# Strassen's seven products in gate/up and fewer of them in down, with h transposed through DRAM and VectorE's work ordered by an estimate of its queue

## The chip, the cores and the metric

The kernel runs on one NeuronCore of a Trainium2 chip. The metric is the device time of one execution in microseconds, lower is better. The time before is the median of three runs.

## The reference

One decoder layer on x with 256 tokens and 2048 features, in float32: a half-step SwiGLU FFN, a mixer (attention and convolution side by side, one projection in and one out), and a second half-step FFN, each followed by a LayerNorm over the residual sum. Cut to what the change touches:

```python
def swiglu_ffn(x, w_gate, w_up, w_down):
    h = jax.nn.silu(x @ w_gate) * (x @ w_up)
    return h @ w_down

x = layer_norm(ALPHA * x + 0.5 * swiglu_ffn(x, gate1, up1, down1), ln1_g, ln1_b)
...
x = layer_norm(ALPHA * x + 0.5 * swiglu_ffn(x, gate2, up2, down2), ln3_g, ln3_b)
```

The hidden width is 5632. Nearly all the arithmetic is in these two FFNs.

## The kernel before, in words

**Precision.** Every float32 operand is split into a high part (a copy rounded to float32r, made by ScalarE) and a low part (the difference, made by VectorE). A product of two operands is three matmuls: high times high, high times low, low times high (`mm3`, lines 547 to 550). The stationary operand is a 128x128 block of activations (features by tokens), the moving one 128x512 of weights.

**Weight tiles.** All weights are read once, in tiles of 128x1024 (512 KB). SyncE (SP) loads them into four `raw` buffers. ScalarE writes `hi` (L204), VectorE `lo` (L207), or GpSimd for some tiles of the mixer. Finished pairs wait in a ring of eight (`RING`); TensorE takes them in order with `take` and frees them with `release`. `ahead` makes tiles up to seven ahead of the one in use (`LEAD`), and is called in `step`, once after every tile's matmuls. The program is written out in one order per engine by this class (`Steps`), so each engine's queue is fixed when the program is built. Work that is due some steps later is put down with `at`. `vector` and `tensor` keep an estimate of VectorE's backlog, which before the change decides only how many taps of the convolution are put in.

**Gate/up.** The hidden columns go in groups of 256 (`JG` = 2 blocks of 128): a tile pair of gate and up columns gives a PSUM bank of 128 tokens by 512 for each of the two token blocks. A group takes 8 tiles, that is 8 K pairs of 256 features: 2 token blocks x 2 K blocks x 3 = 12 matmuls per tile (`token_mm`, `token_group`). There are 22 groups in each FFN, cut into three parts of 8, 8 and 6 groups (`PARTS`), with the down stage of each part behind its gate/up stage. The first two groups of the first FFN are woven (`first_groups`).

**h.** For each group (`group`, lines 818 to 857) ScalarE applies silu, VectorE multiplies (L825), then VectorE transposes 32x32 blocks: four calls of `turn`, one per step, each with four STREAM_TRANSPOSE (L832) that write to other partitions, 16 per group. Then h is split into `hh` and `hl` (L841, L842).

**Down.** In the first two parts (`by_sums`, lines 728 to 807) K pairs are taken for two column chunks at once. Here K pair, two token blocks and two column chunks make 2x2 blocks on each side. A K pair of kind C is done plainly, with 8 products (24 matmuls); one of kind S by Strassen's scheme in Winograd's form, with 7 products of block sums (21 matmuls). `KINDS` gives the kinds: three S of eight. For an S pair the two weight tiles become four ring entries, made by VectorE's sums of blocks (`rest`, lines 159 to 184): the first block pair as it is, two sums, the other tile with one block replaced, and one last sum. The seven products go to seven PSUM banks; VectorE joins them at the end of the stage (`shared`, `add`). The third part uses the plain way for all tiles (`tokens_by`).

Of the kernel before, what the change touches and what calls it, by code (L numbers as in the profile page):

```python
# [18 lines left out]
P = 128  # L19
# [6 lines left out]
KINDS = ("CSCSCSCC", "CSCSCSCC", None)  # L26
BLOCKS = {"S": 7, "C": 4}
JG = 2
# [14 lines left out]
BEHIND = 7  # L43
LAST = 8
# [22 lines left out]
class Steps:  # L67
# [6 lines left out]
    def __init__(self, nc, pool, sources, head, pooled, xT, x_raw, xcat):  # L74
        self.nc, self.pool, self.sources, self.head, self.pooled = nc, pool, sources, head, pooled
        self.xT, self.x_raw, self.xcat = xT, x_raw, xcat
        self.loaded = self.open = self.opened = self.whole = self.done = self.used = self.now = 0
        self.jobs, self.ready, self.pending = [], {}, []
        self.later, self.background, self.backlog = [], None, 0.0
        self.most = len(sources)  # L80
# [23 lines left out]
    def load(self):  # L104
        while self.open < RAW_BUFS and self.loaded < len(self.sources):
            n = self.loaded
            if n < 4:
# [8 lines left out]
            if isinstance(self.sources[n], tuple):  # L116
                if self.opened == 2:
                    return
                self.load_set(n)
                continue  # L120
# [6 lines left out]
    def load_set(self, n):  # L127

        raws = [self.raw(), self.extra.tile([P, 1024], F32, tag="rawx", name=f"rawx{n}", bufs=2)]
        self.opened += 1  # L130
# [3 lines left out]
        self.jobs += [(n, raws, self.first), (n + 3, raws, self.rest)]  # L134

    def upper(self, n, raw):

        pair = [self.pool.tile([P, 1024], F32R, tag=t, name=f"{t}{n}", bufs=RING) for t in ("hi", "lo")]
        hi, lo = (t[:, : raw.shape[1]] for t in pair)
        self.nc.scalar.copy(hi, raw)  # L140

        def lower():
            self.nc.vector.tensor_tensor(out=lo, in0=raw, in1=hi.bitcast(F32), op=ALU.subtract)
            self.vector(1.16, 1.3)
# [10 lines left out]

    def first(self, n, raws):
        raws.append(self.upper(n, raws[0]))

    def rest(self, last, raws):

        n = last - 2
        a, b = ([r[:, :512], r[:, 512:]] for r in raws[:2])
        zero = raws[2]
        sub = self.nc.vector.tensor_tensor
        self.flush(1)
        t = self.extra.tile([P, 1024], F32, tag="sum", name=f"sum{n}", bufs=1)
        sub(out=t[:, :512], in0=b[0], in1=a[0], op=ALU.subtract)
        sub(out=t[:, 512:], in0=b[1], in1=t[:, :512], op=ALU.subtract)
        one = self.upper(n, t)
        sub(out=b[0], in0=b[1], in1=b[0], op=ALU.subtract)  # L170
        two = self.upper(n + 1, raws[1])
        self.flush()
        zero()
        sub(out=a[1], in0=a[1], in1=t[:, 512:], op=ALU.subtract)
        self.vector(2.4, 0.3)
        three = self.upper(n + 2, a[1])

        def ended():
            three()
            self.open -= 1  # L180
            self.opened -= 1
            self.load()

        self.pending = [one, two, ended]

    def split(self):
# [7 lines left out]
        elif n is None:  # L194
            nc.scalar.copy(at[:, :, 0, :], raw)
            nc.vector.tensor_tensor(out=at[:, :, 1, :], in0=raw, in1=at[:, :, 0, :].bitcast(F32), op=ALU.subtract)
        else:
# [19 lines left out]
    def ahead(self, most):  # L217
        while most > 0 and self.jobs:
# [5 lines left out]
            most -= 1  # L224

# [35 lines left out]
    def step(self, us=2.6):  # L261
        self.now += 1
        self.tensor(us)
        for after in (False, True):
# [4 lines left out]
            if not after:  # L269
                self.ahead(2)  # L270
# [5 lines left out]
def hybrid_layer(  # L276
# [8 lines left out]
    act = ctx.enter_context(tc.tile_pool(name="act", bufs=1))  # L285
    psA = ctx.enter_context(tc.tile_pool(name="psA", bufs=2, space=PSUM))
# [6 lines left out]

    def add_ffn(wu, wd):
        for (j0, j1), kinds in zip(PARTS, KINDS):
            for g in range(j0 // JG, j1 // JG):
                sources.extend(wu[g, q, h] for q in range(4) for h in range(2))
            pairs = [divmod(t, 2) for t in range(j0 // 2, j1 // 2)]
            if kinds is None:
                sources.extend(wd[c, g, h] for c in range(NC_) for g, h in pairs)  # L300
                continue
            for c in range(0, NC_, 2):
                for kind, (g, h) in zip(kinds, pairs):
                    both = (wd[c, g, h], wd[c + 1, g, h])
# [1013 lines left out]
```

## Time and profile before

| what | value |
|---|---|
| median of three runs | 1701.65 us (1701.25 to 1701.83) |
| the profiled execution | 1702.42 us |
| its span in the profile | 1700.6 us |
| mean granted clock of TensorE | 0.998 |
| loads from HBM | 332.86 MB, 197 GB/s over the span |
| VectorE: low parts of 1024 columns (L207) | 487 of them, 591.3 us busy |
| VectorE: transposes (L832) | 704, 212.7 us busy |

PE is TensorE, PEld its weight loads, DVE VectorE, ACT ScalarE, POOL GpSimd. Busy time is the time covered by an engine's instruction bars. Where bars overlap, the cost of one instruction is the step from its start to the next start, not the length of its bar. In a row of the groups, "out<-in" are the program's tile names: `grp` is a PSUM bank of gate/up, `sum` one of the products of sums, `acc` one of the plain down way, `xcat` the split x, `hh` and `hl` the split h, `hi` and `lo` the split weights.

### The profile page before, as it was taken

Reading aid. Unit: us, or ns where it says so; the run is one execution under the profiler, and the core shown is the slowest. Engines: PE = TensorE matmul, PEld = TensorE weight load, DVE = VectorE, ACT = ScalarE, POOL = GpSimd, SP = SyncE. Lnnn points to the kernel's source line nnn. Section 1 sums busy time; section 2 is a strip of 40 time slices with the busy share of each in tenths; the row PEclk is TensorE's granted clock in tenths of the full one; section 3 lists DMA queues with packets and bytes.
Section 4 is the critical chain, followed back from the end, with each engine's and each line's share of the span. In section 5 each row is a group of like instructions: output and inputs, shape, how many; then the busy total and the mean of one; then the engine's idle time right before and its main releaser. Section 6 shows DMA issues by size and latency. Waiting matters only on the chain.

```text
span 1700.6 us, 21870 instructions
## 1 busy us (share of the span) xinstructions
PE 1687.1 (99%) x7785; PEld 1402.5 (82%) x7785; DVE 1344.6 (79%) x2305; ACT 847.6 (50%) x1112; POOL 206.3 (12%) x116
## 2 busy tenths in 40 slices
PE   9999999999999999999999999999999999999997
PEld 7888888888888888888888888888888888888886
DVE  6877897777897777658888788988977778977766
ACT  6454454444454444477665465544544444544441
POOL 0000000000000000168996200000000000000000
PEclk9999999999999999999999999999999999999999
DMA  8766467656467566556655557665576664576672
GB/s 307 248 218 209 139 209 238 194 194 204 136 207 247 190 197 194 171 174 190 204 177 160 190 184 240 212 204 169 196 230 190 193 210 159 190 234 197 198 235 75
DMA packets 96303, 336.41 MB, mean 198 GB/s; under 512 B 11200, under 2 KB 11328, under 8 KB 95936
## 3 DMA queue, kind: packets, MB, share of 16 engines
q1 hardware_dynamic: 96048, 334.74, 60.7%
q8 instruction: 61, 1.00, 0.2%
q14 instruction: 50, 0.41, 0.1%
q10 hardware_dynamic: 144, 0.26, 0.0%
HBM read 332.86 MB, written 2.10 MB: 197 GB/s over the span
## 4 chain that ended last, share of the span: by engine, by line
PE 98%; DVE 1%; DMA 0%; issue 0%; ACT 0%; SPq 0%; DVEq 0%
PE grp L549 18%; PE grp L550 18%; PE grp L548 18%; PE sum L548 7%; PE sum L550 6%; PE sum L549 6%; PE acc L548 4%; PE acc L550 4%; PE acc L549 4%; PE in_c L973 2%; PE in_a L973 2%; PE in_q L973 1%; PE in_a L971 1%; PE in_c L971 1%; PE grp L569 1%; PE grp L570 1%
## 5 line engine op out<-in xcount | busy, mean ns | idle before, releaser
L204 ACT CAST hi<-raw 128x1024 fp32r<-128x1024 f32 (+1 forms) x568 | 586.8, 1044 | 474.4 <-PE grp L550 218.0
L207 DVE TENSOR_TENSOR lo<-raw,hi 128x1024 fp32r<-128x1024 f32 (+1 forms) x495 | 596.6, 1219 | 208.9 <-ACT hi L204 204.1
L549 PE MATMUL grp<-lo,xcat 128*128 128x512 f32 x1384 | 538.5, 389 | 0.0
L550 PE MATMUL grp<-hi,xcat 128*128 128x512 f32 x1384 | 538.4, 389 | 0.0
L548 PE MATMUL grp<-hi,xcat 128*128 128x512 f32 x1384 | 538.4, 389 | 0.0
L548 PEld LDWEIGHTS grp<-hi,xcat 128*128 128x128 f32 x1384 | 259.8, 188 | 54.0
L549 PEld LDWEIGHTS grp<-lo,xcat 128*128 128x128 f32 x1384 | 259.8, 188 | 54.0
L550 PEld LDWEIGHTS grp<-hi,xcat 128*128 128x128 f32 x1384 | 259.8, 188 | 53.8
L207 POOL TENSOR_TENSOR lo<-raw,hi 128x1024 fp32r<-128x1024 f32 x73 | 175.7, 2433 | 722.4 <-ACT hi L204 715.5
L832 DVE STREAM_TRANSPOSE hf<-ht 32x128 f32<-32x128 f32 x704 | 212.7, 302 | 11.0
L548 PE MATMUL sum<-hi,hh 128*128 128x512 f32 x488 | 189.9, 389 | 0.0
L549 PE MATMUL sum<-lo,hh 128*128 128x512 f32 x488 | 189.9, 389 | 0.0
L550 PE MATMUL sum<-hi,hl 128*128 128x512 f32 x488 | 189.9, 389 | 0.0
L550 PEld LDWEIGHTS sum<-hi,hl 128*128 128x128 f32 x488 | 91.6, 188 | 19.2
L549 PEld LDWEIGHTS sum<-lo,hh 128*128 128x128 f32 x488 | 91.6, 188 | 18.9
L548 PEld LDWEIGHTS sum<-hi,hh 128*128 128x128 f32 x488 | 91.6, 188 | 18.9
L1036 DVE SCALAR_TENSOR_TENSOR conv<-hc,cw_sb,conv 128x256 f32<-128x256 f32 x231 | 96.7, 485 | 1.1
L841 ACT CAST hh<-hf 128x512 fp32r<-128x512 f32 (+1 forms) x44 | 26.0, 592 | 128.3 <-DVE hf L832 128.3
L531 POOL TENSOR_SCALAR rs_t<-rs_y,rs_w 128x1 f32<-128x1 f32 x1 | 0.3, 342 | 711.4 <-DVE rs_y L530 711.4
L548 PE MATMUL acc<-hi,hh 128*128 128x512 f32 (+1 forms) x196 | 75.8, 387 | 0.9 <-DVE st L387 0.8
L550 PE MATMUL acc<-hi,hl 128*128 128x512 f32 (+1 forms) x196 | 75.6, 385 | 0.0
L549 PE MATMUL acc<-lo,hh 128*128 128x512 f32 (+1 forms) x196 | 75.4, 385 | 0.0
(174 smaller groups left out, 1527.6 us busy)
## 6 DMA issues: line engine op xcount, KB each, us to landing
raw<-in_wu SPq DMA_DIRECT2D x348, 512.0 KB, 4.3
raw<-in_wd SPq DMA_DIRECT2D x152, 512.0 KB, 4.2
raw<-in_win SPq DMA_DIRECT2D x52, 512.0 KB, 4.1
raw<-in_wout SPq DMA_DIRECT2D x32, 512.0 KB, 3.7
rawx<-in_wd SPq DMA_DIRECT2D x24, 512.0 KB, 6.5
xt<-in_xT SPq DMA_DIRECT2D x8, 256.0 KB, 5.6
raw<-in_head SPq DMA_DIRECT2D x8, 256.0 KB, 5.8
xt<-in_x SPq DMA_DIRECT2D x2, 1024.0 KB, 7.1
```

The lines of the kernel that those rows point to most:

```text
L204: nc.scalar.copy(hi, raw)
L207: eng.tensor_tensor(out=lo, in0=raw, in1=hi.bitcast(F32), op=ALU.subtract)
L548: nc.tensor.matmul(ps, s_hi, m_hi, start=start, stop=False)
L549: nc.tensor.matmul(ps, s_hi, m_lo, start=False, stop=False)
L550: nc.tensor.matmul(ps, s_lo, m_hi, start=False, stop=stop)
L569: nc.tensor.matmul(ps, lhs[0][at], w[0][:, n], start=k == 0, stop=False)
L570: nc.tensor.matmul(ps, lhs[0][at], w[1][:, n], start=False, stop=False)
L832: nc.vector.transpose(dst[:, t], src[:, f])
L841: nc.scalar.copy(hi, src)
L971: nc.tensor.matmul(ps[:, :S], w[1][:, n], x1[:, k, 0, :], start=False, stop=k == KT - 1)
L973: nc.tensor.matmul(ps, w[0][:, n], x1[:, k], start=k == 0, stop=False)
L1036: nc.vector.scalar_tensor_tensor(out=out, in0=x_, scalar=w, in1=acc, op0=ALU.mult, op1=ALU.add)
```

## The change

**Gate/up by pairs of groups.** From the third group on, two groups (512 hidden columns) are done together by the same `by_sums`, now with the blocks, the joining and the output passed in. `UP` orders the eight K pairs: K pairs 0 and 1 (`SUMMED`) are of kind S, the other six of kind C. The four sums of blocks of x that an S pair needs are made once per FFN (`sums_of`, tile `xs`). At the end of a pair of groups four joining additions (`shared`) and four more (`out`) bring the seven banks and the plain products into four SBUF tiles `part`; then silu and the gate products follow from there.

**Down.** `KINDS` has two S of eight instead of three, in another order. The third part takes the last pair's tiles of the first two column chunks later (`down_order`).

**h through DRAM.** Per four blocks of hidden columns, one STREAM_TRANSPOSE of 128x1024 turns all 32x32 blocks in place of the 32 small ones. GpSimd's queue then writes the result to a DRAM tile `far` in four DMAs of 128 KB and reads it back in one DMA of 512 KB in the order that puts features on partitions (`turn`). The rows of the down weights are laid out to match (`turned`). The low parts of h are queued six steps later.

**VectorE's order.** In these stages (`paced`) tiles are no longer made per step but per product: `pace` lowers the estimated backlog by 0.68 after each product and adds VectorE work until the estimate is at least 1.2. Small work that can wait is kept in `soon` and put in when three tiles are in stock. During the last four products of a stage nothing is put in. The set of an S pair is made in four jobs (`zeroth`, `first`, `second`, `third`) instead of two. The residual work of the second FFN and the load of x get other steps.

On PE, in the first FFN's third group: each tile is multiplied with both token blocks, 12 matmuls. (`hi19` and `lo19` are the parts of tile 19, `grp0` and `grp1` the banks of the two token blocks.)

```order
L548 MATMUL grp0_549<-hi19_455,xcat0_78 128x512
L549 MATMUL grp0_549<-lo19_456,xcat0_78 128x512
L550 MATMUL grp0_549<-hi19_455,xcat0_78 128x512
L548 MATMUL grp0_549<-hi19_455,xcat0_78 128x512
L549 MATMUL grp0_549<-lo19_456,xcat0_78 128x512
L550 MATMUL grp0_549<-hi19_455,xcat0_78 128x512
L548 MATMUL grp1_550<-hi19_455,xcat0_78 128x512
L549 MATMUL grp1_550<-lo19_456,xcat0_78 128x512
L550 MATMUL grp1_550<-hi19_455,xcat0_78 128x512
L548 MATMUL grp1_550<-hi19_455,xcat0_78 128x512
L549 MATMUL grp1_550<-lo19_456,xcat0_78 128x512
L550 MATMUL grp1_550<-hi19_455,xcat0_78 128x512
```

In the changed program, in the first pair of groups, these are the last four of the seven products of the first S pair, three matmuls each. (Entries 20 to 23 are one set, `xs` the sums of x, `sum_564` to `sum_568` PSUM banks.)

```order
L624 MATMUL sum_564<-hi22_534,xs_144 128x512
L625 MATMUL sum_564<-lo22_535,xs_144 128x512
L626 MATMUL sum_564<-hi22_534,xs_144 128x512
L624 MATMUL sum_566<-hi20_497,xcat0_80 128x512
L625 MATMUL sum_566<-lo20_498,xcat0_80 128x512
L626 MATMUL sum_566<-hi20_497,xcat0_80 128x512
L624 MATMUL sum_567<-hi23_588,xcat0_80 128x512
L625 MATMUL sum_567<-lo23_589,xcat0_80 128x512
L626 MATMUL sum_567<-hi23_588,xcat0_80 128x512
L624 MATMUL sum_568<-hi22_534,xs_144 128x512
L625 MATMUL sum_568<-lo22_535,xs_144 128x512
L626 MATMUL sum_568<-hi22_534,xs_144 128x512
```

A set holds the weights of two tiles and is used for 21 matmuls; two plain tiles are used for 24.

On VectorE, in the second and third group of the first FFN before: gate products, low parts of tiles and the transposes in between.

```order
L825 TENSOR_TENSOR ht_533<-sl_535,grp_146 128x256
L825 TENSOR_TENSOR ht_533<-sl_538,grp_146 128x256
L207 TENSOR_TENSOR lo23_564<-raw23_459,hi23_563 128x1024
L832 STREAM_TRANSPOSE hf_534<-ht_533 32x2x2x32 x4
L207 TENSOR_TENSOR lo24_586<-raw24_481,hi24_585 128x1024
L832 STREAM_TRANSPOSE hf_534<-ht_533 32x2x2x32 x4
L207 TENSOR_TENSOR lo25_608<-raw25_503,hi25_607 128x1024
L832 STREAM_TRANSPOSE hf_534<-ht_533 32x2x2x32 x4
L207 TENSOR_TENSOR lo26_630<-raw26_525,hi26_629 128x1024
L832 STREAM_TRANSPOSE hf_534<-ht_533 32x2x2x32 x4
```

After the change, behind the first pair of groups (`part` are the joined sums, `hr` the turned h, `sum45` the two sums of blocks of a set):

```order
L949 TENSOR_TENSOR ht_936<-part_780 128x8x32
L963 STREAM_TRANSPOSE hr_941<-ht_936 128x1024
L171 TENSOR_TENSOR sum45_965<-rawx44_859,raw44_858 128x512
L171 TENSOR_TENSOR sum45_966<-rawx44_859,sum45_965 128x512
L171 TENSOR_TENSOR rawx44_859<-rawx44_859 128x512
L157 TENSOR_TENSOR lo44_963<-raw44_858,hi44_962 128x1024
L171 TENSOR_TENSOR raw44_858<-raw44_858,sum45_966 128x512
L157 TENSOR_TENSOR lo45_970<-sum45_965,hi45_969 128x512
L157 TENSOR_TENSOR lo45_970<-sum45_966,hi45_969 128x512
L157 TENSOR_TENSOR lo46_981<-rawx44_859,hi46_980 128x1024
L157 TENSOR_TENSOR lo47_992<-raw44_858,hi47_991 128x512
```

and, with three low parts between, what uses the data that come back from DRAM (`hf`) at the end of the same pair:

```order
L157 TENSOR_TENSOR lo51_1055<-raw51_1010,hi51_1054 128x1024
L977 TENSOR_TENSOR hl0_146<-hf_948,hh0_145 128x512
L926 TENSOR_TENSOR sums_1074<-hf_948 128x128 x2
L926 TENSOR_TENSOR sums_1074<-sums_1074,hf_948 128x128
L926 TENSOR_TENSOR sums_1074<-hf_948,sums_1074 128x128
L977 TENSOR_TENSOR hl0_146<-hf_948,hh0_145 128x384
L977 TENSOR_TENSOR hl0_146<-sums_1074,hh0_145 128x512
L157 TENSOR_TENSOR lo52_1090<-raw52_1025,hi52_1089 128x1024
L1002 TENSOR_TENSOR part_1101<-sum_908,part_1100 128x512
```

The 32 small transposes of two groups are one row; sums and low parts of sets stand where plain low parts stood, and the use of `hf` stands 14 rows behind the transpose. The diff, cut to its core:

```diff
-KINDS = ("CSCSCSCC", "CSCSCSCC", None)
+KINDS = ("SCCSCCCC", "SCCSCCCC", None)
+UP = (
+    ((2, "C"), (3, "C"), (0, "S"), (4, "C"), (1, "S"), (5, "C"), (6, "C"), (7, "C")),
+    ((0, "S"), (2, "C"), (3, "C"), (1, "S"), (4, "C"), (5, "C"), (6, "C"), (7, "C")),
+)
+SUMMED = (0, 1)
+AHEAD = 1.2
+PACE = 0.68
+STOCK = 3
...
+    def pace(self, us, ending=False):
+        self.tensor(us)
+        while self.backlog < AHEAD and not ending:
+            more = self.can() or self.pending
+            if self.soon and (not more or self.whole - self.used >= STOCK):
+                self.soon.pop(0)()
+            elif self.can():
+                self.split()
+            elif self.pending:
+                self.flush(1)
+            else:
+                break
...
+    def by_sums(kinds, blocks, out, shared):
...
+        def product(k, x_, w, half):
+            cols = slice(half * 512, (half + 1) * 512)
+            left[k] -= 1
+            mm3(bank[k], *x_, w[0][:, cols], w[1][:, cols], left[k] == uses[k] - 1, left[k] == 0)
+            st.pace(PACE, ending[0])
...
+                u = [st.take() for _ in range(2)]
+                product(1, at("11"), u[0], 0)
+                product(5, at("S1"), u[1], 0)
+                product(6, at("S2"), u[1], 1)
+                u.append(st.take())
+                product(7, at("S3"), u[2], 0)
+                st.step(0)
+                product(2, at("12"), u[0], 1)
...
+                product(4, at("22"), u[3], 0)
+                product(3, at("S4"), u[2], 1)
...
+                    hr = pool.tile([P, 4, 2 * P], F32, tag="ht", name="hr")
+                    nc.vector.transpose(hr.rearrange("p f n -> p (f n)"), ht.rearrange("p f j b n -> p (f j b n)"))
+                    st.vector(1.25)
+                    far = dram.tile([4, 32, 4, 2 * P], F32, tag="far", name="far")
+
+                    for t in range(4):
+                        nc.gpsimd.dma_start(far[:, :, t].rearrange("f r n -> r f n"), hr[32 * t : 32 * t + 32])
+                    hf = pool.tile([P, 8 * P], F32, tag="ht", name="hf")
+                    nc.gpsimd.dma_start(hf, far.rearrange("f r t n -> (f r) (t n)"))
...
+                    st.at(6, lambda: st.soon.extend([lambda t=t: split(hf, t) for t in range(2)]))
...
+                def pair(g, ups):
...
+                    def shared(bank):
+
+                        tmp.extend(act.tile([P, 512], F32, tag="z", name="part", bufs=ZB) for k in range(4))
+                        nc.scalar.copy(tmp[0], bank[1])
+                        add(tmp[1], bank[6], tmp[0])
+                        add(tmp[2], bank[5], tmp[1])
+                        add(tmp[1], bank[7], tmp[1])
+                        add(tmp[3], bank[5], tmp[1])
+
+                    def out(at, ps):
+
+                        y = tmp[places[at]]
+                        add(y, ps, y)
+                        nc.scalar.activation(y[:, : JG * P], y[:, : JG * P], AF.Silu)
...
-        x2, "2", BEHIND, lambda: residuals(par2, 3, None, nc.vector, 4, 6), prepare3,
+        x2, "2", BEHIND, lambda: residuals(par2, 3, None, nc.vector, 12,10), prepare3,
```

More of the change, by code (lines that the diff above doesn't have):

```diff
@@ L115, in load @@
                 continue
[L116 to L120, printed above, removed]
             raw = self.raw()
@@ L180, in ended @@
             self.open -= 1
-            self.opened -= 1
+            self.sets -= 1
             self.load()
-        self.pending = [one, two, ended]
+        self.pending.append(ended)
     def split(self):
@@ L196, in split, with ended @@
             nc.vector.tensor_tensor(out=at[:, :, 1, :], in0=raw, in1=at[:, :, 0, :].bitcast(F32), op=ALU.subtract)
+        elif self.paced and raw.shape[1] == 1024:
+            lower = self.upper(n, raw)
+            self.flush()
+            self.jobs.pop(0)
+            def ended():
+                lower()
+                self.open -= 1
+                self.load()
+            self.pending.append(ended)
         else:
@@ L268, in step @@
                 x[2]()
-            if not after:
+            if not after and not self.paced:
+                self.drain()
                 self.ahead(2)
@@ L673, in tokens_by @@
         half = nk // 2
-        order = [(c, t) for c in range(NC_) for t in range(half)]
+        order = down_order(nk)
         skew = 0 if finish is None else SKEW if kept is None else LAST
@@ new lines, in by_sums @@
+    def by_sums(kinds, blocks, out, shared):
+        one, seven = (p.tile([P, 512], F32, tag="acc", name="sum") for p in (psB, psC))
+        mid = psA.tile([P, 2, 512], F32, tag="gu", name="sum")
+        two, four = (p.tile([P, 512], F32, tag="acc", name="sum") for p in (psB, psC))
+        end = psA.tile([P, 2, 512], F32, tag="gu", name="sum")
+        bank = {1: one, 7: seven, 5: mid[:, 0], 6: mid[:, 1], 2: two, 4: four, 3: end[:, 0], 0: end[:, 1]}
+        final = kinds.rindex("S")
+        uses = {k: kinds.count("S") for k in (1, 5, 6, 7)}
+        uses |= {k: kinds.count("S") + 2 * kinds.count("C") for k in (2, 3, 4)} | {0: 2 * kinds.count("C")}
+        left, ending = dict(uses), [False]
+        def product(k, x_, w, half):
[3 more added lines that the diff above has]
+            st.pace(PACE, ending[0])
+        for n, kind in enumerate(kinds):
+            if kind == "S":
+                at = lambda name, n=n: blocks(n, name)
+                u = [st.take() for _ in range(2)]
[6 more added lines that the diff above has]
+                product(2, at("12"), u[0], 1)
+                st.release()
+                st.release()
+                u.append(st.take())
+                product(4, at("22"), u[3], 0)
+                product(3, at("S4"), u[2], 1)
+                st.release()
+                st.release()
+                if n == final:
+                    st.drain()
+                    shared(bank)
+                st.step(0)
+                continue
+            for i, (p, q) in enumerate(((2, 4), (3, 0))):
+                w = st.take()
+                for k, row, at in ((p, "1", (0, i)), (q, "2", (1, i))):
+                    ending[0] = n == len(kinds) - 1 and k in (3, 0)
+                    for half in range(2):
+                        product(k, blocks(n, row + "12"[half]), w, half)
+                    if n == len(kinds) - 1 and i == 0:
+                        out(at, bank[k])
+                if n == len(kinds) - 1 and i == 1:
+                    for k, at in ((p, (0, i)), (q, (1, i))):
+                        out(at, bank[k])
+                st.release()
+                st.step(0)
@@ new lines, in parted, with split @@
+                        st.vector(src.shape[1] * 0.13 + 0.08)
+                    def split(hf, t):
+                        full = hf.rearrange("p (t k i) -> p k t i", t=4, k=8)
+                        if kinds is None:
+                            return parted(8 * g + 4 * t, full[:, 4 * t : 4 * t + 4])
+                        kind = kinds[2 * g + t]
+                        at = sum(BLOCKS[k] for k in kinds[: 2 * g + t])
+                        some = full[:, 4 * t : 4 * t + 4]
+                        if kind == "C":
+                            return parted(at, some)
+                        sums = act.tile([P, 4, P], F32, tag="z", name="sums", bufs=ZB)
+                        view = sums.rearrange("p k (t i) -> p k t i", t=4)
+                        block_sums(view, [some[:, k] for k in range(4)])
+                        parted(at, some[:, 1:])
+                        parted(at + 3, sums)
```

342 lines of the change are left out of this document (185 added, 157 removed).

## The prediction

> **What bounds the kernel now.** I read the page first: the busy table and the chain that ended last.
>
> ```profile
> span 1700.6 us, 21870 instructions
> PE 1687.1 (99%) x7785; PEld 1402.5 (82%) x7785; DVE 1344.6 (79%) x2305; ACT 847.6 (50%) x1112; POOL 206.3 (12%) x116
> PE 98%; DVE 1%; DMA 0%; issue 0%; ACT 0%; SPq 0%; DVEq 0%
> ```
>
> TensorE (PE) is busy for 99% of the span and is 98% of the chain. A busy PE could still hide waits, since its bars are pipelined. So I read who PE waited for (engine, line, what for, total us, times, longest):
>
> ```profile
> PE grp L642 <- ACT hi L204: 1.6, 2, 1.1
> PE idle L327 <- DVE ones L324: 1.2, 1, 1.2
> PE acc L548 <- DVE st L387: 0.8, 1, 0.8
> ```
>
> That is all: 3.6 us, at the start and in the tail. What one matmul costs is not its bar of 389 ns but the step from start to start. It is read from the PE timeline, here in a gate/up stage (grp) and in a down stage that already uses products of sums (sum):
>
> ```profile
> 299.68 0.39 PE L549 MATMUL grp<-lo,xcat 128*128 128x512 f32 x1
> 299.90 0.39 PE L550 MATMUL grp<-hi,xcat 128*128 128x512 f32 x1
> 300.13 0.39 PE L548 MATMUL grp<-hi,xcat 128*128 128x512 f32 x1
> ...
> 305.57 0.39 PE L548 MATMUL grp<-hi,xcat 128*128 128x512 f32 x1
> ```
>
> ```profile
> 228.05 0.39 PE L548 MATMUL sum<-hi,hh 128*128 128x512 f32 x1
> ...
> 228.73 0.39 PE L548 MATMUL sum<-hi,hh 128*128 128x512 f32 x1
> ```
>
> From 300.13 to 305.57 there are 24 matmuls, so one takes 5.44 / 24 = 0.2267 us. In the sums three take 228.73 - 228.05 = 0.68, which is the same. So a product of sums costs PE what any product of that shape costs, and a matmul that disappears is worth 0.2267 us as long as nothing else makes PE wait.
>
> What could make it wait is VectorE (DVE), which makes the low parts. The windows view gives busy time by stage; DVE's is the third of the busy numbers. The first two rows are a down and a gate/up stage of the first FFN, the last a down stage of the second:
>
> ```profile
> 200.00:250.00 50.00, 50.00 (x222) 41.43 (x221) 47.44 (x56) 26.62 (x29) 0.00 (x0) 1.00 0.57 190
> 300.00:350.00 50.00, 50.00 (x223) 41.39 (x221) 36.77 (x62) 22.12 (x27) 0.00 (x0) 1.00 0.64 197
> 1450.00:1500.00 50.00, 50.00 (x222) 41.43 (x221) 47.36 (x57) 27.75 (x30) 0.00 (x0) 1.00 0.61 202
> ```
>
> In the down stage DVE is busy for 95% of the window and PE still loses nothing. The ring of eight finished weight tiles carries PE over it. ScalarE (ACT) has half its time free, GpSimd (POOL) all of it, and the granted clock is 1.00.
>
> **PE's part of the sum.** A K pair that goes by seven products takes 21 matmuls for two weight tiles where the plain way takes 24. Gate/up has 22 groups per FFN. The first two stay plain, the other 20 form 10 pairs of groups, each with 2 K pairs by products: 10 x 2 x 3 = 60 matmuls fewer. Down has two parts with two pairs of column chunks, each with 2 instead of 3 K pairs by products: 2 x 2 x 1 x 3 = 12 more. Net 48 fewer in each FFN, 96 in the kernel, and 96 x 0.2267 = 21.8 us. Nothing is added to PE: the transposes of h were DVE's and stay off PE, and the sums of x are made on DVE and ACT.
>
> [...]
>
> **DVE's part.** It decides whether the 21.8 us can be collected. I need steps, not bars, because DVE's bars overlap too:
>
> ```profile
> 205.73 3.49 DVE L207 TENSOR_TENSOR lo<-raw,hi 128x1024 fp32r<-128x1024 f32 x3
> 220.02 0.68 DVE L167 TENSOR_TENSOR sum<-rawx,raw 128x512 f32<-128x512 f32 x1
> 220.74 0.69 DVE L168 TENSOR_TENSOR sum<-rawx,sum 128x512 f32<-128x512 f32 x1
> 221.35 0.69 DVE L170 TENSOR_TENSOR rawx<-rawx 128x512 f32<-128x512 f32 x1
> 221.95 1.22 DVE L143 TENSOR_TENSOR lo<-raw,hi 128x1024 fp32r<-128x1024 f32 x1
> 306.68 0.41 DVE L825 TENSOR_TENSOR ht<-sl,grp 128x256 f32<-128x256 f32 x1
> 309.69 1.24 DVE L832 STREAM_TRANSPOSE hf<-ht 32x128 f32<-32x128 f32 x4
> 318.97 0.49 DVE L851 TENSOR_TENSOR ht<-hf 128x128 f32<-128x128 f32 x2
> 319.91 0.55 DVE L842 TENSOR_TENSOR hl<-hf,hh 128x384 fp32r<-128x384 f32 x1
> ```
>
> Three low parts of 1024 columns take 3.49, the last with its whole bar of 1.22, as in the row at 221.95: (3.49 - 1.22) / 2, or 1.13 each. One of 512 columns takes 221.35 - 220.74 = 0.61, or 220.74 - 220.02 = 0.72 where it reads the result ahead of it; the gate product 0.41; four small transposes 1.24, so 0.31 each; a sum of 128 columns 0.2 (two in 0.49).
>
> Now one pair of groups after the change, 186 matmuls x 0.2267 = 42.2 us of PE:
> - 6 plain K pairs, 12 tiles x 1.13 = 13.6
> - 2 K pairs by products, each two low parts of 1024 and seven operations of 512 (four sums, three low parts): 2 x (2.26 + 4.27) = 13.1
> - joining the banks, eight additions of 512: 4.9
> - four gate products: 1.6
> - one transpose of 128x1024, which no row shows: from 1.13 (a subtraction of that width) to 8 x 0.31 = 2.5 (eight of the small ones, 128 columns each). I take 1.25, near the lower end: sums of 128 columns take 0.2 each and the subtraction of 1024 not 8 x 0.2 but 1.13, so wide operations save most of the starts.
> - low parts of h: 0.6 for a plain K pair, about 2.0 for one by products (four sums, 0.55, 0.6); with 2 of 8 by products 2 x (0.25 x 2.0 + 0.75 x 0.6) = 1.9
>
> Together 36.4 us, 86%. The removed work is large: 32 small transposes per two groups, 32 x 0.31 = 9.9 us, become one.
>
> The down stage after the change is 42.2 us of PE again with 12 x 1.13 + 13.1 + 12 x 0.61 = 34.0 us of DVE, 81%. Before, by the same steps: 10 x 1.13 + 3 x 6.4 + 7.3 = 37.8 us beside 183 x 0.2267 = 41.5, 91%. So the densest stage of the change asks less of DVE than a stage that the trace shows running without a wait of PE.
>
> The new order costs DVE some idle time. While PE makes the last four products of a stage (4 x 0.68 = 2.7 us) nothing new is queued, so that the joining additions start at once. That is from 0 (the queue still covers it) to 2.7 us per pair; I take 2. Even 36.4 + 2.7 = 39.1 is under 42.2. In the second FFN's first part the residual work adds 16 x 0.61 = 9.8 us over three pairs, 3.3 per pair: 36.4 + 2.7 + 3.3 = 42.4 at the worst, 0.2 us over in each of three pairs. The ring covers that: DVE may be seven tiles ahead, which is 7 x 2.72 = 19 us of plain tiles, or 13 where a product set (four tiles, 4.8 us) is among them. I cost it at nothing; without that cover it is under 1 us.
>
> ACT and the loads have room:
>
> ```profile
> L204 ACT CAST hi<-raw 128x1024 fp32r<-128x1024 f32 x560 | 581.8, 1050 | 472.0 <-PE grp L550 218.0 <-PE acc L550 89.3 <-DMA raw<-in_wu 58.6
> L140 ACT CAST hi<-raw 128x512 fp32r<-128x512 f32 x24 | 14.9, 622 | 13.6 <-DVE raw L174 8.9 <-PE grp L550 4.8
> raw<-in_wu SPq DMA_DIRECT2D x348, 512.0 KB, 4.3
> rawx<-in_wd SPq DMA_DIRECT2D x24, 512.0 KB, 6.5
> ```
>
> A pair takes ACT 16 casts x 1.05 and some 14 smaller ones x 0.62, about 25 us of 42. Weights are the same bytes, 512 KB per 2.6 us; the road through DRAM adds 1 MB per 42 us, an eighth.
>
> **The road through DRAM.** Per pair POOL issues four writes of 128 KB and one read of 512 KB. The trace has no DMA from POOL's queue. Nearest rows: 4.3 us for a 512 KB load, 6.5 for one that is queued behind another. Two in a row, 8.6 to 13; I take 11. What reads the result is queued six steps behind the transpose, and a step is 2.1 to 2.7 us of PE: about 15 us. So it lands in time. The tightest place is the third part, where the last pair's h is wanted after eight tiles, 8 x 2.72 = 21.8 us into down. The gate runs one step in (2.7), gate and transpose end at about 6, the data land at about 17 and casting and low part take 2 more: 19 of 21.8.
>
> **The sum.** The profiled execution took 1702.42 us with a span of 1700.6; the median of the runs is 1701.65. 1700.6 - 21.8 = 1678.8 of span. By the median, 1701.65 - 21.8 = 1679.9; I say 1680.
>
> **The rivals.**
> *DVE comes up short.* [...] Chance 10%.
> *The h data come back too late: slower than before.* DVE works in order; a low part of h that waits for its DMA holds every weight tile behind it. The ring then feeds PE for the 13 us above, so this decides from a round trip of 15 + 13 = 28 us on. There are 11 turns in each FFN; at 29.5 us each of the 22 costs PE 1.5, 33 in all: 1713. For it: nothing in the trace shows how POOL's queue does; against it: the rows put two trips at 8.6 to 13 us. Chance 5%.
> [...]
> *The order is wrong at stage ends.* The change sets DVE's order by an estimate. If it puts a tile that waits for a ring slot ahead of a joining addition, the bank is freed late and the next stage's product waits. 28 stage ends at 0.7 us, a quarter of a tile, are 20 us: 1700, no change. Against it: the change stops queueing there, and a bank is wanted 2.7 us or later after its last product. Chance 4%. That the work does not shrink is no case: 21 matmuls against 24 are in the program.
>
> **How the numbers follow.** The forecast, 1680, has 77%, between 1678.5 and 1683 (the transpose at its dear end, a us or two in the residual part or at the third parts). The rivals in their order have 10% (1683 to 1692), 5% (slower) and 4% (1692 to 1704), and 4% is left for what I don't see, half of it slower. The low end is 1678.5: 21.8 is all that goes, and PE has only 3.6 us of waits to lose. The forecast's own band leaves out more than 2 in 10, so the range reaches into the first rival, to 1690. Faster or slower counts from 0.2% (3.4 us), about what a measurement of this kernel can tell from no change: faster by more 90%, within 3%, slower by more 7%.
>
> **What would show it.** PE has 96 matmuls fewer and still steps at 0.2267; its waits stay under 5 us in all. DVE in the gate/up windows rises from 37 to about 45 of 50, and falls in down from 47 to about 43. One transpose bar near 1.3 us. From transpose to landing 8 to 13 us, and no long wait of DVE for hf. I am wrong if PE waits for lo in every pair (DVE short), for hl or lo behind a DMA (the road), or at the first products of a stage (banks).

## The result

The changed kernel takes 1688.13 us (median of four runs, 1687.06 to 1688.99), the kernel before 1701.66 in the same comparison. The ratio is 0.9921, 95% interval 0.9903 to 0.9938. The forecast was 1680.0 with a range of 1678.5 to 1690. So the change is faster, as forecast, but 13.5 us of the 21.8 came and some 8 are missing. Where these are is the question of the rest.

### The profile page after: what moved, and what is told of

Its sections match the earlier page's. It is cut to its first block, busy times and chain, and to the rows that moved or that the text cites. A ratio compares the mean times of both kernels' runs of the same rounds, so it can differ in the third digit from the quotient of the medians.

```text
span 1687.2 us, 21755 instructions
## 1 busy us (share of the span) xinstructions
PE 1669.7 (99%) x7689; PEld 1383.6 (82%) x7689; DVE 1386.7 (82%) x2035; ACT 912.9 (54%) x1252; POOL 268.1 (16%) x226
## 3 DMA queue, kind: packets, MB, share of 16 engines
q1 hardware_dynamic: 96048, 334.74, 58.6%
## 4 chain that ended last, share of the span: by engine, by line
PE 67%; DVE 19%; DMA 6%; issue 5%; ACT 3%; DVEq 0%; POOL 0%; ACTq 0%; SPq 0%; POOLq 0%
PE sum L624 13%; PE sum L625 13%; PE sum L626 13%; DVE lo L157 9%; PE acc L624 4%; PE acc L626 4%; PE acc L625 4%; DMA raw<-in_wu 3%; ACT hi L153 2%; DVE part L1002 2%; DVE sum L171 2%; PE in_c L1149 2%; PE in_a L1149 2%; PE in_q L1149 1%; DMA raw<-in_wd 1%
## 5 line engine op out<-in xcount | busy, mean ns | idle before, releaser
L157 DVE TENSOR_TENSOR lo<-raw,hi 128x1024 fp32r<-128x1024 f32 x452 | 506.6, 1153 | 121.5 <-ACT hi L153 121.0
L153 ACT CAST hi<-raw 128x1024 fp32r<-128x1024 f32 x452 | 432.9, 996 | 298.9 <-DMA raw<-in_wu 108.1
L624 PE MATMUL sum<-hi,xcat 128*128 128x512 f32 x1080 | 420.4, 389 | 1.6 <-DVE part L1002 1.6
L625 PE MATMUL sum<-lo,xcat 128*128 128x512 f32 x1080 | 420.3, 389 | 0.6 <-DVE lo L157 0.6
L626 PE MATMUL sum<-hi,xcat 128*128 128x512 f32 x1080 | 420.2, 389 | 0.0
L624 PEld LDWEIGHTS sum<-hi,xcat 128*128 128x128 f32 x1080 | 202.7, 188 | 44.7 <-DVE part L1002 2.5
L625 PEld LDWEIGHTS sum<-lo,xcat 128*128 128x128 f32 x1080 | 202.7, 188 | 42.9 <-DVE lo L157 1.0
L626 PEld LDWEIGHTS sum<-hi,xcat 128*128 128x128 f32 x1080 | 202.7, 188 | 42.2
L236 ACT CAST hi<-raw 128x1024 fp32r<-128x1024 f32 (+1 forms) x164 | 166.6, 1030 | 119.9 <-PE acc L626 71.8
L153 ACT CAST hi<-sum 128x512 fp32r<-128x512 f32 x112 | 69.5, 622 | 139.1 <-DVE sum L171 128.9
L239 DVE TENSOR_TENSOR lo<-raw,hi 128x1024 fp32r<-128x1024 f32 (+1 forms) x91 | 106.9, 1203 | 37.9 <-ACT hi L236 37.1
L1002 DVE TENSOR_TENSOR part<-sum,part 128x512 f32<-128x512 f32 x160 | 105.1, 685 | 12.7 <-PE sum L626 8.1
## 6 DMA issues: line engine op xcount, KB each, us to landing
far<-hr POOLq DMA_DIRECT2D x88, 128.0 KB, 2.7
```

The costliest lines, as they stand in the source:

```text
L153: self.nc.scalar.copy(hi, x_)
L157: self.nc.vector.tensor_tensor(out=lo, in0=x_, in1=hi.bitcast(F32), op=ALU.subtract)
L239: eng.tensor_tensor(out=lo, in0=raw, in1=hi.bitcast(F32), op=ALU.subtract)
L624: nc.tensor.matmul(ps, s_hi, m_hi, start=start, stop=False)
L625: nc.tensor.matmul(ps, s_hi, m_lo, start=False, stop=False)
L626: nc.tensor.matmul(ps, s_lo, m_hi, start=False, stop=stop)
```

## The profile after

The page, busy time and the chain that ended last:

```profile
span 1687.2 us, 21755 instructions
PE 1669.7 (99%) x7689; PEld 1383.6 (82%) x7689; DVE 1386.7 (82%) x2035; ACT 912.9 (54%) x1252; POOL 268.1 (16%) x226
PE 67%; DVE 19%; DMA 6%; issue 5%; ACT 3%; DVEq 0%; POOL 0%; ACTq 0%; SPq 0%; POOLq 0%
```

PE has its 96 matmuls fewer and is still busy for 99%. But the chain is no longer PE's: a third of it goes over other engines, 6% over DMA. Who PE waits for (engine, line, what for, total us, times, longest):

```profile
PE sum L624 <- DVE part L1002: 2.9, 4, 0.9
```

This row is new: a product waits for a joining addition, `part`, that has to free its bank. These waits are understated, since a matmul's bar is 0.39 us long and steps are 0.2267. The loss is read from the starts. PE's timeline at the stage boundaries (a stage of gate/up ends where `xcat` gives way to `hh`), with one long gap behind the end of a pair of groups (the pair's last matmul is the one at 133.33) and one stretch without a wait:

```profile
49.17 0.39 PE L624 MATMUL sum<-hi,xcat 128*128 128x512 f32 x1
...
133.33 0.39 PE L626 MATMUL sum<-hi,xcat 128*128 128x512 f32 x1
...
136.05 0.39 PE L626 MATMUL sum<-hi,xs 128*128 128x512 f32 x1
137.16 0.50 PE L624 MATMUL sum<-hi,xcat 128*128 128x512 f32 x1 [0.72 <-DVE part L1002]
...
177.15 0.39 PE L624 MATMUL sum<-hi,hh 128*128 128x512 f32 x1
...
263.19 0.39 PE L624 MATMUL sum<-hi,xcat 128*128 128x512 f32 x1
...
299.91 0.39 PE L624 MATMUL sum<-hi,xcat 128*128 128x512 f32 x1
305.35 0.39 PE L624 MATMUL sum<-hi,xcat 128*128 128x512 f32 x1
...
431.82 0.39 PE L624 MATMUL sum<-hi,hh 128*128 128x512 f32 x1
516.14 0.39 PE L624 MATMUL sum<-hi,xcat 128*128 128x512 f32 x1
642.62 0.39 PE L624 MATMUL acc<-hi,hh 128*128 128x512 f32 x1
...
1013.92 0.39 PE L624 MATMUL sum<-hi,xcat 128*128 128x512 f32 x1
1143.44 0.39 PE L624 MATMUL sum<-hi,hh 128*128 128x512 f32 x1
1229.90 0.39 PE L624 MATMUL sum<-hi,xcat 128*128 128x512 f32 x1
```

From 299.91 to 305.35 there are 24 matmuls, 5.44 / 24 = 0.2267 each as before. Three pairs of groups have 3 x 186 = 558 matmuls, 126.48 us of PE; two down stages 372, 84.32. Measured, in the order of the stages of the first FFN: 127.98, 86.04, then (four pairs, 744 matmuls, 168.64) 168.63, 84.32, 126.48. In the second FFN the first part takes 129.52 and 86.46. So the first part loses 1.50 + 1.72 in the first FFN and 3.04 + 2.14 in the second, 8.4 us in all. The parts behind lose nothing in the first FFN and 0.5 in the second, in the second part's down (84.83 us). Together 8.9 us: 21.8 - 8.9 = 12.9, beside 13.4 between the two spans.

DVE's busy time by stage, the third busy number, in the windows shown of before and in the first part of the second FFN:

```profile
200.00:250.00 50.00, 49.87 (x220) 40.84 (x219) 44.23 (x56) 27.37 (x32) 0.00 (x0) 1.00 0.67 235
300.00:350.00 50.00, 50.00 (x223) 41.39 (x221) 42.43 (x56) 26.09 (x37) 2.77 (x5) 1.00 0.63 216
1100.00:1150.00 50.00, 47.87 (x207) 37.91 (x206) 45.46 (x60) 28.45 (x40) 2.77 (x5) 1.00 0.71 234
1450.00:1500.00 50.00, 50.00 (x222) 41.40 (x222) 43.31 (x52) 26.45 (x30) 0.00 (x0) 1.00 0.62 209
```

Down fell from 47 to 43 or 44, gate/up rose from 37 to between 42 and 45 (the window from 1100 holds 6.6 us of down as well). DVE is never full, not where PE waits for it either. It is late there with time left over.

What it was late for shows in the chain, followed back through the first part (start, length, what):

```profile
72.50 1.23 DVE lo L157
73.74 5.00 DMA raw<-in_wu
78.82 1.06 ACT hi L153
79.90 1.23 DVE lo L157
...
108.32 3.50 DVE lo L157 x3
111.83 5.76 DMA raw<-in_wu
```

A low part ends and frees a `raw` buffer; only then does the load of a later tile start; cast and low part of that tile wait for it. ScalarE's waits for loads, 58.6 us for `in_wu` and 20.3 for `in_wd` before (line L204), are now:

```profile
ACT hi L153 <- DMA raw<-in_wu: 110.5, 48, 5.0
ACT hi L153 <- DMA raw<-in_wd: 81.0, 49, 4.6
```

## The experiments

Each kernel is the changed kernel with the edit shown. Theory A at first: DVE falls behind in the first parts, because extra work lies there. Theory B: weights come late behind the road through DRAM. Theory C: the order at the ends of stages is wrong by itself.

**The extra work moved to GpSimd.** In the second FFN's first part lies the residual work on DVE, in the first FFN's the scaling of x by ScalarE, two bars of 1.91 us (L427) among the casts.

```diff
e1: -residuals(par2, 3, None, nc.vector, 12,10)
e1: +residuals(par2, 3, None, nc.gpsimd, 12,10)
e2: -nc.scalar.mul(xt[:, b], xt[:, b], ALPHA)
e2: +nc.gpsimd.tensor_scalar(out=xt[:, b], in0=xt[:, b], scalar1=ALPHA, scalar2=None, op0=ALU.mult)
e3: both
```

Expected of the first, the second and both:

> The residual work of the second FFN's first part (16 operations of 512 columns) goes to GpSimd in place of VectorE. Theory A (VectorE is behind at stage ends in the first part of each FFN because of work beside the FFN's own; the joining additions then come late and TensorE waits): the waits of TensorE in the second FFN's first part, 5.1 us over its gate/up and down stages, fall to 2 or less, those of the first FFN stay near 3.2, and the time falls by 2 to 5 us, to about 1684. Theory B (weights come later because the road through DRAM and the loads share the DMA engines): no change, 1688. Theory C (the order at stage ends is wrong by itself): no change in either FFN.

> The two scalings of the token rows (2048 columns each, 1.9 us each on ScalarE between the weight casts of the first FFN's first part) go to GpSimd; the two 1 MB loads stay where they are. Theory A: TensorE's waits in the first FFN's first part fall from 3.2 us to 2 or less, the second FFN's stay at 5, time about 1686. Theory B: the loads are what hurts, no change. Theory C: no change.

> Both moves together. Theory A: TensorE's waits in both first parts nearly vanish, 1680 to 1683, which is the forecast. Theory B: 1687 to 1688. Theory C: 1687 to 1688.

Measured: 1691.57, 1693.60 and 1696.14 us; ratios to before 0.9938 [0.9925, 0.9950], 0.9952 [0.9939, 0.9964] and 0.9968 [0.9956, 0.9981]. No move brought the 2 to 8 us that theory A gave it. The second and third kernel are slower than the changed one; of the first that can't be said by its time alone, since its runs (from 1688.61) touch those of the changed kernel. But the stage whose work was moved is what got slower in each: with the residual on GpSimd the second FFN's first part takes 131.38 and 88.81 instead of 129.52 and 86.46, with the scaling there the first FFN's 131.43 and 86.36 instead of 127.98 and 86.04. What got in the way stands in the timelines of the second kernel, DVE's and GpSimd's:

```profile
128.30 4.12 DVE L171 TENSOR_TENSOR rawx<-rawx 128x512 f32<-128x512 f32 x1
```

```profile
127.73 5.88 POOL L427 TENSOR_SCALAR xt<-xt 128x2048 f32<-128x2048 f32 x1 [20.58 <-DMA xt<-in_x]
```

A subtraction of 512 columns, 0.69 us in every row so far, takes 4.12 while GpSimd works on x. In the first kernel five low parts in a row take 9.32 us (from 1115.71) beside three such instructions of GpSimd; four took 4.09 in the changed kernel. The work was taken off one engine and stood in the way of DVE from another. The test says nothing for or against A, since it gave DVE no time.

**The work left out.** The first kernel leaves out the residual work of the second FFN's first part, the second the scaling of x, so their outputs differ from the reference's.

```diff
f1: -residuals(par2, 3, None, nc.vector, 12,10)
f1: +None
f2: -st.at(4, lambda: nc.scalar.mul(xt[:, b], xt[:, b], ALPHA))
```

> The residual work of the second FFN's first part is left out (the token rows are not normalised and scaled there, so the last residual sum is another): 16 operations of VectorE, 16 scalings of ScalarE and eight row loads fewer. Theory A (VectorE is behind there because of work beside the FFN's own): the second FFN's first part, 129.5 us of gate/up and 86.5 of down against 126.5 and 84.3 of bare matmuls, loses its 5.2 us of waits down to under 1; time 1683. Theory C (the order at stage ends is wrong by itself): at least 3 of the 5 us stay, 1686 to 1688.

> The two scalings of the token rows on ScalarE in the first FFN's first part are left out (the residual sum is then of the unscaled rows); the loads of the rows stay. Theory A, with ScalarE's 1.9 us between the casts as the cause: the first FFN's first part, 128.0 + 86.0 us, falls to 126.5 + 84.3, time 1685. If the 2 MB of loads in the weights' queue are the cause: no change there, 1688.

Measured: 1685.16 us (0.9904 [0.9890, 0.9919]) and 1686.02 (0.9910 [0.9895, 0.9925]). PE's timeline of the kernel without the residual work, second FFN:

```profile
1014.53 0.39 PE L624 MATMUL sum<-hi,xcat 128*128 128x512 f32 x1
...
1141.01 0.39 PE L624 MATMUL sum<-hi,hh 128*128 128x512 f32 x1
...
1227.10 0.39 PE L624 MATMUL sum<-hi,xcat 128*128 128x512 f32 x1
```

Gate/up takes 126.48: the 3.0 us of that stage are gone to the last tenth. Its down takes 86.09 and keeps 1.8 of its 2.1 us, where I had expected under 1 us for the whole part; that loss is not the residual work's. Without the scaling the first FFN's first gate/up stage takes 126.48 as well (48.86 to 175.34), and its down 84.97. So the gate/up stage of each first part loses by its own extra work. In the first FFN this is work of ScalarE alone. In the second it isn't parted: the residual work that was left out is 20 instructions of DVE, 12 of ScalarE and eight loads of rows. That ScalarE's 3.8 us in 128 cost 1.5 us there was not explained by A: ScalarE has nearly half of its time free there (it is busy for 70.27 of 128 us in the changed kernel).

**Parts of the change undone.** No queue estimate and tiles made once per step (e4; the new condition never holds), transposes by DVE alone (e5), one K pair of kind S instead of two in gate/up (e6):

```diff
e4: -while self.backlog < AHEAD and not ending:
e4: +while self.background == 1:
e4: -st.paced = True
e4: +st.paced = False
e5: +for f in range(4):
e5: +    for t in range(4):
e5: +        nc.vector.transpose(hf[32*f : 32*f+32, 256*t : 256*t+256], src[:, f])
e6: -(1, "S")
e6: +(1, "C")
```

(In e5 these 16 calls stand for hr, far and the five DMAs; `src` are the 32 partitions of `ht` from 32 t on.)

> Work for VectorE is put in once per step again, as before the change, with no estimate of its queue; everything else as in the change. Theory C (the estimate's order makes the waits): as fast as the change or faster, 1680 to 1688. Theories A and B: the joining additions come behind more tiles and the small work is not held back, so TensorE waits in more stages, 1692 to 1710.

> h is turned by 16 small transposes of 32x256 per turn on VectorE, as it was done before, with no road through DRAM; the order is that of the change. One small one should take 0.45 us by its columns, 7.1 per turn in place of 1.25. If VectorE is what limits the gate/up stages (36.4 us + waits of 42.2 per pair): 5.9 us more per pair is more than is free, TensorE then waits in every gate/up stage, 1 to 4 us per pair: 1710 to 1750. If VectorE has room and the road through DRAM is what delays weights (theory B): 1680 to 1690.

> One K pair by products in gate/up in place of two: 3 x 10 x 2 = 60 matmuls more for TensorE, 13.6 us, and 4.3 us less for VectorE per pair of groups. If TensorE's waits come from VectorE's load (theory A), they vanish: 1688 + 13.6 - 8 = 1694. If they come from the order at stage ends (theory C) or from the loads (B), they stay: 1701 to 1702.

Measured: e4 1733.50 us (1.0191 [1.0175, 1.0207]); e5 1793.77 (1.0545 [1.0530, 1.0561]); e6 1696.04 (0.9971 [0.9959, 0.9982]). The largest row of PE's waits in e4:

```profile
PE sum L624 <- DVE part L1002: 22.5, 11, 3.1
```

The order by the queue estimate, with all that hangs on it, is worth 45 us, more than any theory had: without it the joining additions stand behind tiles, and PE waits up to 3.1 us for one.

Without the road through DRAM the kernel is 106 us slower: 16 transposes of 32x256 at 0.436 us are 7.0 us per pair instead of 1.25, and every pair then runs over PE's time (three pairs take 143.9, not 126.5). I had expected 1710 to 1750, from 1 to 4 us per pair; the first parts lose 6 to 7 per pair, and each of the four stages of down by sums loses 6 to 8 as well. The 106 are not the price of the work alone: each small transpose was entered in the queue estimate with 0.078 us, 1.25 per pair, so the order was made for less work than DVE had. No run parts the two.

In e6 the gate/up stages of three pairs take 128.5, which is 3 x 189 x 0.2267 and no more, and the two first downs lose 0.2 and 2.5 us. That is near A's 1694 and far from C's and B's 1701: with one set less per pair, and 4.3 us less of DVE's work, gate/up loses nothing. In e5 there is no road, a load of weights takes 4.6 and 4.8 us in the median (4.8 and 4.7 in the changed kernel), and ScalarE still waits 89.0 and 74.2 us for weights; so weights do come late, but not by the road, as B has it.

**More products of sums, and other places in the order.** Three of eight in down as before the change (e7), three in gate/up (e8), and the changed kernel with the block sums no longer followed at once by their own low part and the scaling of x in four pieces (g2):

```diff
e7: -KINDS = ("SCCSCCCC", "SCCSCCCC", None)
e7: +KINDS = ("SCCSCSCC", "SCCSCSCC", None)
e8: -SUMMED = (0, 1)
e8: +SUMMED = (0, 1, 2)
g2: -        self.pending.append(self.upper(n, raws[1]))
g2: -        self.flush(1)
g2: +        lower = self.upper(n, raws[1])
g2: +        self.flush(1)
g2: +        self.pending.append(lower)
g2: -            elif self.pending:
g2: +            elif len(self.pending) > 1:
g2: +        for c in range(NC_):
g2: +            y = xt[:, b, c * 512 : (c + 1) * 512]
g2: +            st.at(4 + c, lambda y=y: nc.scalar.mul(y, y, ALPHA))
```

> Three of the eight K pairs of down by products of sums again, gate/up left as in the changed kernel. PE has 2 FFNs x 2 parts x 2 pairs of column chunks x 3 = 24 matmuls fewer, 24 x 0.2267 = 5.4 us: 1688.1 - 5.4 = 1682.7 if VectorE's slack in down is not needed. Theory A (VectorE falls behind in gate/up and the down stages give the time back): a down stage's work rises from 34.0 to 37.8 us beside 41.5 of PE, and the low parts of h by 1.4 us per part, so it gives back some 4 us less, and a part of the 5.4 is lost, above all in the second parts, which start with more lag: 1684 to 1688. Theory C (the order at stage ends costs a fixed time by itself): 1682.7 within 1.

> Three K pairs instead of two by products of sums in each pair of groups. PE has 20 x 3 = 60 matmuls fewer, 13.6 us: 1674.5 if PE alone counted. VectorE gets 6.5 - 2.3 = 4.3 us more per pair of groups: 40.7 of work beside 41.5 of PE. Theory A (beside its work VectorE stands idle for some 5 us per pair of groups): 45.7 beside 41.5, 4 us over in each of 20 pairs less some 5 that the ring takes per part: 1700 to 1730, with PE waiting for lo and for the joining additions in every pair. If only the work counted and the 2.7 us at the end of a stage (my prediction's terms): 43.4 beside 41.5, 1.9 over in each, less the ring's part: 1676 to 1695. Theory C: about 1675.

> Same work as the changed kernel, two changes of order: a block sum is no longer followed at once by its own low part (20 of 22 such places go; there VectorE waits for ScalarE's cast), and the scaling of x on ScalarE is done in four pieces of 512 columns instead of one of 2048. Theory A, with these waits as the idle time that fills VectorE's pairs of groups: VectorE's lag at the ends of stages grows less, and most of the 3.2 and 3.0 us of the first parts' gate/up comes back: 1682 to 1685. If the waits only move to another place (VectorE is held by ScalarE's casts anyway, or by the ring): 1686 to 1688.

Measured: e7 1749.78 us (1.0284 [1.0270, 1.0298]), e8 1809.81 (1.0634 [1.0614, 1.0655]), g2 1688.43 (0.9925 [0.9912, 0.9937]). None of my theories had e7 or e8 in its range. g2 speaks against A in the form that DVE's waits for casts are the loss: they fall from 134.7 to 46.7 us, and the time stays. They moved in part, to waits for `hh` (56.0 us). The first gate/up stage takes 128.08 as before; the down behind it loses nothing now, and the second FFN's first part loses 7.7 us in place of 5.2. So another order in the middle of a stage moves the loss and doesn't remove it. g2 was not aimed at the order at the ends of stages, and of C it says little.

e7 points to the cause. It has less PE work than the changed kernel, and each down by sums takes 8 to 10 us more than its matmuls (and each gate/up stage behind one 7 to 10), while DVE is idle more. Its window, in the first FFN's down, and then ScalarE's and DVE's timelines there:

```profile
200.00:250.00 50.00, 45.04 (x181) 35.03 (x180) 39.40 (x50) 23.13 (x28) 0.00 (x0) 0.93 0.48 168
```

```profile
234.15 1.05 ACT L153 CAST hi<-raw 128x1024 fp32r<-128x1024 f32 x1 [3.60 <-DMA raw<-in_wd]
```

```profile
238.72 0.69 DVE L171 TENSOR_TENSOR sum<-rawx,raw 128x512 f32<-128x512 f32 x1 [2.26 <-DMA rawx<-in_wd]
```

DVE is busy for 39 of 50 us and the DMA engines for 48%, while PE, ScalarE and DVE wait for loads. Neither work nor bandwidth is short. What may be short is the number of loads under way.

**Theory D: the round of the four raw buffers.** A `raw` buffer is loaded (4.8 us in the median), waits for its cast (1.05), waits for its low part (1.13) and is free. That is 7.0 us without the waits. Four buffers at 2.72 us of PE per tile allow 10.9, so the waits have 3.9 us. A set of an S pair holds one of the four until its last low part. Whatever makes the cast or the low part later, on ScalarE or on DVE, makes the next load later by the same time. To test it I gave the ring a fifth buffer, and took the room from the mixer:

```diff
-RAW_BUFS = 4
+RAW_BUFS = 5
-HB = 5
+HB = 4
-pT = pool.tile([P, 2, 3 * P], F32, tag="pT", name="pT", bufs=2)
+pT = pool.tile([P, 2, 3 * P], F32, tag="pT", name="pT", bufs=1)
```

> Five buffers for raw weight tiles instead of four (the room comes from the mixer, one transposed-probabilities buffer and one convolution buffer fewer; what the mixer may lose by that, 0 to 3 us, is read apart). No instruction of the FFNs is added or taken away. Theory D, formed from the chain in the first part of the changed kernel (low part, then DMA of the next raw tile 4.3 to 7 us, then cast, then low part): VectorE stands idle because a raw buffer comes round too slowly. Four buffers at 2.72 us of PE per tile come round every 10.9 us, of which load, cast and low part take 4.8 + 1.05 + 1.13 = 7.0, and a set holds one of the four for longer. With five it is 13.6. Then ScalarE's waits for loads of weights (110.5 and 81.0 us) fall by half or more, the lag of the joining additions stays under 5 us and the FFNs lose at most 2 of the 8.8 us: 1680 to 1683 plus the mixer's loss. Theory A in its first form (VectorE's own work, the pause at the ends of stages and its exchanges with ScalarE fill the time, whatever is loaded): the lag and the losses stay, 1686 to 1690.

Measured: 1684.40 us (1683.93 to 1684.51), ratio 0.9898 [0.9881, 0.9914]; all its runs are under all those of the changed kernel. Page (the chain), PE's and ScalarE's waits and PE's timeline:

```profile
PE 98%; DVE 1%; DMA 0%; ACT 0%; issue 0%; SPq 0%; DVEq 0%; ACTq 0%
```

```profile
PE tp L1310 <- ACT pT L1300: 3.8, 4, 1.0
```

```profile
ACT hi L153 <- DMA raw<-in_wu: 17.0, 23, 2.0
...
ACT hi L153 <- DMA raw<-in_wd: 8.9, 18, 1.8
```

```profile
49.19 0.39 PE L624 MATMUL sum<-hi,xcat 128*128 128x512 f32 x1
...
175.67 0.39 PE L624 MATMUL sum<-hi,hh 128*128 128x512 f32 x1
...
259.99 0.39 PE L624 MATMUL sum<-hi,xcat 128*128 128x512 f32 x1
...
706.51 0.39 PE L649 MATMUL grp<-hi,xcat 128*128 128x512 f32 x1
...
969.94 0.40 PE L649 MATMUL grp<-hi,xcat 128*128 128x512 f32 x1
...
1015.66 0.39 PE L624 MATMUL sum<-hi,xcat 128*128 128x512 f32 x1
1142.14 0.39 PE L624 MATMUL sum<-hi,hh 128*128 128x512 f32 x1
1226.46 0.39 PE L624 MATMUL sum<-hi,xcat 128*128 128x512 f32 x1
```

The first parts take 126.48, 84.32, 126.48 and 84.32: exactly what the matmuls cost. All 8.9 us are back, with the same work on every engine of the FFNs. ScalarE's waits for loads fall from 191.5 to 25.9 us, and the chain is PE's again. In the first FFN, DVE's 739 and ScalarE's 455 instructions stand in the same order in both traces, and a load takes no less time (4.9 us in the median); the loads only start earlier. So neither the order nor the work is the cause of the 8.9 us, and the number of buffers is: with four, the extra work of the first parts costs time, with five the same work costs none. What the run doesn't gain it pays in the mixer, from 706.51 to 969.94, 263.4 instead of 258.5 us, more than the 0 to 3 that I had expected. PE waits there 3.8 us for `pT`, whose second buffer was taken; no run took the mixer's buffers alone. 1684.4 - 4.9 = 1679.5 would be the time without that, an estimate, since no run has both.

The same place of the joining additions, in DVE's timeline of the changed kernel and of this one:

```profile
136.43 2.48 DVE L1002 TENSOR_TENSOR part<-sum,part 128x512 f32<-128x512 f32 x4
```

```profile
131.31 1.28 DVE L1002 TENSOR_TENSOR part<-sum,part 128x512 f32<-128x512 f32 x2
133.71 1.29 DVE L1002 TENSOR_TENSOR part<-sum,part 128x512 f32<-128x512 f32 x2 [1.12 <-PE sum L626]
```

The pair's last matmul starts at 133.33 with four buffers and at 133.28 with five. With four the additions begin 3.1 us behind that; with five two of them begin 2.0 us ahead, and the other two wait for PE.

## Why the prediction was right, and where it was not

The measured time lies in the range, but outside the forecast's own band, which ends at 1683. The range reaches to 1690 for the first rival alone, and that rival is not what happened: that 1688 lies within the range is luck.

**PE's part** was right: 96 matmuls fewer at 0.2267.

**DVE's work** was right in gate/up. Over three pairs of groups of the changed kernel:

```profile
49.00:177.00 128.00, 127.15 (x560) 104.48 (x559) 109.19 (x142) 70.27 (x89) 10.45 (x18) 1.00 0.67 230
```

109.19 / 3 = 36.4, as summed. The wide transpose, which no row of before showed, is 1.245 us; I took 1.25. Down is busy for 43 of 50, as forecast for the window, though the sum of 34.0 in 42.2 would be 40 of 50. About 3 us per pair of column chunks are missing from that sum, among them what the last pair of groups leaves over: additions, gate products, its transpose and low parts of h.

**The idle time and the cover** failed. I took 2 us of idle time per pair; the row shows (128.0 - 109.2) / 3 = 6.3. And I costed the residual work at nothing because the ring of eight finished tiles would cover it, "7 x 2.72 = 19 us". The ring can cover only if it is full, and here it filled no faster than raw buffers came round. The step that failed is "ACT and the loads have room": I counted ScalarE's busy time and the bytes per us, and both do have room, but not the round of a buffer against the number of buffers. The trace of before had the numbers: 4.3 us per load, casts of 1.05, low parts of 1.13, and ScalarE already waiting 78.9 us for weights. The scaling of x, 2 x 1.91 us on ScalarE, I didn't cost at all. Nor did I cost the residual work's 12 instructions on ScalarE. The residual work, at nothing or "under 1 us" in the text, is worth 3.9 us in the second FFN (5.7 lost with it, 1.8 without); all that the cover was to hide is 8.9. The mark for PE's waits was 5 us in all; the view of waits has 5.9, the starts of the matmuls 8.9.

**The road through DRAM** came in time, and the long wait for `hf` isn't there: ScalarE waits for it 3.9 us in all, DVE 0.4. In the first pair the transpose ends at 101.70 (100.45 and 1.25). GpSimd's timeline and the issues (KB each, median us to landing):

```profile
101.99 2.25 POOL L968 DMA_DIRECT2D far<-hr  x4 [36.30 <-DVE hr L963]
106.83 0.57 POOL L970 DMA_DIRECT2D hf<-far  x1 [2.59 <-DMA far<-hr]
```

```profile
far<-hr POOLq DMA_DIRECT2D x88, 128.0 KB, 2.7
hf<-far POOLq DMA_DIRECT2D x22, 512.0 KB, 3.6
```

106.83 + 3.6 - 101.70 = 8.7 us with the median for the read, at the short end of 8.6 to 13. The last pair of the third part was in time, too: its down takes 67.1 us, from 642.62 to 709.70, exactly as long as before the change.

**The rivals.** 1688 lies in the band of the first rival, DVE coming up short (1683 to 1692), and it is not that rival. The band stands for 0.4 us lost in each of 20 pairs, with each of DVE's instructions costing its whole bar, and no run shows that term: the second and third parts lose nothing in gate/up, and three low parts still take 3.50 (row at 108.32), steps of (3.50 - 1.22) / 2 = 1.14 beside a bar of 1.22. The rival's first half is true, DVE comes late; the reason is its supply. The third rival's mechanism, a bank freed late by a joining addition, is how the loss is paid (the row of PE's waits), but the order isn't the cause: h1 has the same order and brings the time back.

**What stays open.** That e7's and e8's great losses are the raw buffers too is argued from the waits; none was run with five, nor was e4. How long a raw buffer's round really is was not measured either: that waits and sets fill the 10.9 us is inferred from h1. What the down of the second FFN's first part loses by without the residual work (1.8 us) was not read. Nor is it settled why down with three of eight ran without a loss before, with four buffers: there a set was made in two jobs, and a load of `in_wd` took 4.2 us in the median instead of e7's 4.9. And ScalarE's waits for loads are no measure of the loss by themselves: e6 has more of them (184.0 us for `in_wu`) and loses 2.7 us.

## What to carry to other kernels

A ring of finished tiles is only a cover if what stands ahead of it can fill it. Beside busy time and bytes, work out for each ring of buffers the round of one buffer (load, wait, first use, wait, last use) against the buffers times the time per tile, and ask what holds a buffer longer. Where an engine is late and idle at once, look in the chain for the transfer whose start it releases.

## What the runs showed of the hardware

In e2 a DVE subtraction of 512 columns took 4.12 us beside a GpSimd instruction of 5.88, and 0.69 in the kernel before (row at 221.35). Moving the residual work from DVE to GpSimd took the gate/up stage it lies in from 129.52 to 131.38 us; moving the scaling of x to it from ScalarE took its stage from 127.98 to 131.43.

The granted clock was lower where PE waited much: 0.93 in e7's window above, where PE stands still for an estimated 9 of 50 us (181 matmuls at 0.2267 are 41.0), and 0.982 over the whole of e5, against 0.998 in the changed kernel. At the end of that stage of e7 three steps from matmul to matmul, from 269.35 to 270.03, still take 0.68, or 0.227 us each.
